# Three of four softmax-weight scalings moved from VectorE to GpSimd in a hybrid HGRN2/NSA decoder trunk

## The chip, the core and the metric

The kernel runs on one core of a Trainium2 chip, in float32 throughout. A core has a matmul engine (TensorE, PE in the profile, with its weight loads as PEld), VectorE (DVE), ScalarE (ACT), GpSimd (POOL), and SyncE (SP), which here only issues transfers. Each engine runs its own instructions in the order in which the program gives them, and waits on semaphores for what the others make. The metric is the device time of one execution in microseconds.

## The reference

Two layers, 512 tokens of width 1024. Each layer has a token mixer of two head groups (a gated linear recurrence, "HGRN2", and native sparse attention, "NSA"), an output product with a residual and a layer norm, and a SwiGLU feed-forward block with a second norm. The change lies in NSA. Cut to that:

```
for l in range(DEPTH):
    proj = x @ w_in[l]
    hq, hf, hi, hg, nq, kc, vc, ks, vs, kw, vw, gt = split(proj)
    o_a = hgrn2_mixer(hq, hf, hi, hg, ...)                 # 4 heads
    # NSA: 8 query heads, 2 key/value groups, gates g0, g1, g2 = sigmoid(gt) per head
    p_c = masked_softmax(q kc'^T * scale + bias)           # compressed blocks
    p_s = masked_softmax(q ks^T * scale + bias)            # selected blocks: all of them, as S = 512
    p_w = masked_softmax(q kw^T * scale + bias)            # sliding window
    o_b = g0 * (p_c @ vc') + g1 * (p_s @ vs) + g2 * (p_w @ vw)
    x = layer_norm(ALPHA * x + concat(o_a, o_b) @ w_out[l])
    x = layer_norm(ALPHA * x + (silu(x @ w_gate) * (x @ w_up)) @ w_down)
```

## The kernel before

Every large product is made of three fp32r products (a value is split into a rounded part and the rest: `whi`/`wlo`, `xh`/`xl`), at lines 82 to 84, with ScalarE making the rounded part and VectorE the rest (lines 76 and 77). These are most of TensorE's work.

NSA runs in 16 steps per layer (`nsa_all`): 8 heads times two branches, b = 0 for the selected blocks and b = 1 for the window. Of a step, `nsa_scores` makes the scores of four tiles of 128 tokens (qt = 0 to 3, 128, 256, 384 and 512 keys wide) on TensorE (lines 622 to 626, into `ps_s`), adds the bias from a strip and takes the minimum on VectorE (line 611), exponentiates and sums on ScalarE (line 613), and then makes the factor `sm`, one number per token and tile: the reciprocal of the sum (line 631) times the gate (line 632). The weights are scaled by it, three tiles on VectorE (line 635) and the widest on ScalarE (line 637). `nsa_pv` transposes the scaled weights on TensorE in groups of 4, 3 and 3 (line 652, into `ps_t`), ScalarE rounds each group (line 656), VectorE makes the rest (line 657), and TensorE multiplies both by the values (lines 662 and 663, into `ps_o`). `nsa_fin` ends a head.

The weights live in tiles named `e`: `e13` and `e2` of each step and `e0` of each head, two buffers each. So the scores of step i + 2 can be written by VectorE only when the transposes of step i are done.

Between the steps lie, called from `nsa_all` by step, other work: dense products with x (projections for the later heads and the linear recurrence, tiles `xh`, `xl`), the levels of the recurrence (`hg_levels`, with a GpSimd copy at line 392 on each level), its outputs (`hg_out`, lines 450 to 465, with a power on GpSimd at line 457), and at the end the first products of the output projection (`first_half`, `second_half`). GpSimd also issues transfers: the bias strips (line 328), residual rows (line 871), and sums of feed-forward weights (lines 104 and 105).

The order of the instructions on each engine is set when the program is built, by the tile framework's scheduler from priorities and its own estimates of durations; at run time nothing is reordered. A changed instruction can therefore move many others.

Of the kernel before, what the change touches and what calls it, by code (L numbers as in the profile page):

```python
# [13 lines left out]
OP = mybir.AluOpType  # L14
# [20 lines left out]
class Kern:  # L35
# [556 lines left out]
    def nsa_scores(self, h, b):  # L592
        nc = self.nc
        g = h // 4
        q = self.QS[h]
        KH, KL = self.KHL
        if b == 0:
            self.st = self.strip(h)
        st = self.st
        es = self.sb.tile([128, 1024], F32, name="e13", tag="e", bufs=2)  # L600
        e1, e3 = es[:, :512], es[:, 512:]
        e2 = self.sb.tile([128, 256], F32, name="e2", tag="e2", bufs=2)
        if b == 0:

            self.e0 = self.sb.tile([128, 128], F32, name="e0", tag="e0", bufs=2)
            self.mnsm = [(self.small(4, "mn"), self.small(4, "sm")) for _ in range(2)]
        E = [e1[:, 0:128] if b == 0 else self.e0, e2, e1[:, 128:512], e3]
        mn, sm = self.mnsm[b]

        def soft(e, pa, mn, sm):  # L610
            nc.vector.tensor_tensor_reduce(out=e, in0=pa, in1=st[:, 512 - pa.shape[-1]:], scale=1.0, scalar=3e38,  # L611
                                           op0=OP.add, op1=OP.min, accum_out=mn)
            nc.scalar.activation(e, e, AF.Exp, bias=mn, scale=-1.0, accum_out=sm)  # L613

        for qt in range(4):
            n = 128 * (qt + 1)
            qq = q[:, qt * 128:(qt + 1) * 128]
            if qt == 0:
                p0 = self.ps("s")
                if b == 0:  # L620
                    for i, k in enumerate((KH, KL)):
                        nc.tensor.matmul(p0[:, 256:], qq, k[:, g::2, :128], start=i == 0, stop=i == 1)
                continue
            p = p0[:, :n] if qt == 1 else self.ps("s")[:, :n]
            nc.tensor.matmul(p, qq, KH[:, 2 * b + g, :n], start=True, stop=False)
            nc.tensor.matmul(p, qq, KL[:, 2 * b + g, :n], start=False, stop=True)  # L626
            if qt == 1 and b == 0:
                soft(E[0], p0[:, 256:384], mn[:, :1], sm[:, :1])
                soft(self.e0, p0[:, 384:], self.mnsm[1][0][:, :1], self.mnsm[1][1][:, :1])
            soft(E[qt], p, mn[:, qt:qt + 1], sm[:, qt:qt + 1])  # L630
        nc.vector.reciprocal(sm, sm)
        nc.vector.tensor_tensor(sm, sm, self.gt[:, :, 8 * (b + 1) + h], op=OP.mult)
        for qt in range(4):
            if qt < 3:
                nc.vector.tensor_scalar(E[qt], E[qt], sm[:, qt:qt + 1], None, op0=OP.mult)
            else:
                nc.scalar.activation(E[qt], E[qt], AF.Copy, scale=sm[:, qt:qt + 1])
        self.E[h, b] = E
# [691 lines left out]
```

## Time and profile before

| | us |
|---|---|
| median of 3 runs | 1336.96 (1335.33 to 1340.11) |
| the profiled execution | 1336.99 |
| its span, first to last instruction | 1335.2 |
| TensorE busy in the span | 1303.4 (98%) |
| VectorE busy | 1015.6 (76%) |
| ScalarE busy | 748.0 (56%) |
| GpSimd busy | 186.5 (14%) |

The profiled execution's own time exceeds its span by 1.8 us. Its granted TensorE clock is 0.995 of full speed as a mean. In the profile a matmul's row is longer than the time until the next one may start, so a busy TensorE is not one at its peak. Engines run side by side, so the shares don't add up.

### The profile page before, as it was taken

The page shows a single profiled execution, that of the slowest core. Times are in us where ns is not written, and L with a number is a line of the kernel's source. Part 1 is how long each engine was busy: PE and PEld are TensorE (multiplying, and loading weights), DVE is VectorE, ACT ScalarE, POOL GpSimd, SP SyncE. Part 2 cuts the span into 40 slices and gives each one's busy share as a digit, 9 for nine tenths or more (in the row PEclk, how much of TensorE's full clock was granted, in tenths as well). Part 3 has the DMA queues.
Part 4 walks back from the last instruction along what each step waited for, and adds up shares of the span by engine and source line. Part 5 has one row for each costly group of instructions (what it writes and reads, how often), then busy time and mean ns, then how long its engine had stood idle before and what let it go on. Part 6 is the DMA issues. An engine that isn't in the chain of part 4 may idle for free.

```text
span 1335.2 us, 23431 instructions
## 1 busy us (share of the span) xinstructions
PE 1303.4 (98%) x8853; PEld 1197.8 (90%) x8853; DVE 1015.6 (76%) x2024; ACT 748.0 (56%) x1492; POOL 186.5 (14%) x267
## 2 busy tenths in 40 slices
PE   8999999999999999999999999998999999999997
PEld 6988999788999999888899989997899999998886
DVE  4755798867698777978758668988568887789777
ACT  5244787844655555645353558777356555556640
POOL 1140110110011212020011100101101112211102
PEclk9999999999999999999999999999999999999999
DMA  7253212162277888495433221123424778965952
GB/s 230 88 163 106 72 48 71 56 209 79 78 174 187 227 237 205 121 230 153 157 140 102 95 87 64 63 65 110 135 80 135 174 200 215 242 174 128 229 179 79
DMA packets 67554, 186.54 MB, mean 140 GB/s; under 512 B 8047, under 2 KB 8223, under 8 KB 66928
## 3 DMA queue, kind: packets, MB, share of 16 engines
q1 hardware_dynamic: 44640, 124.73, 28.1%
q0 software_dynamic: 21792, 58.47, 21.1%
q10 hardware_dynamic: 1008, 1.84, 0.4%
q8 instruction: 69, 1.13, 0.3%
q14 instruction: 45, 0.37, 0.1%
HBM read 180.76 MB, written 7.10 MB: 141 GB/s over the span
## 4 chain that ended last, share of the span: by engine, by line
PE 87%; DVE 5%; DMA 2%; ACT 2%; issue 2%; POOL 1%; POOLq 0%; DVEq 0%; ACTq 0%
PE ps_d L82 16%; PE ps_d L83 16%; PE ps_d L84 15%; PE ps_t L82 4%; PE ps_t L84 4%; PE ps_t L83 4%; PE ps_s L83 3%; PE ps_s L84 3%; PE ps_s L82 3%; PE ps_t L652 2%; PE ps_h L395 2%; PE ps_o L663 1%; PE ps_o L662 1%; PE ps_s L524 1%; PE ps_o L84 1%
## 5 line engine op out<-in xcount | busy, mean ns | idle before, releaser
L116 ACT CAST whi<-wraw 128x512 fp32r<-128x512 f32 x160 | 98.7, 621 | 127.5 <-PE ps_d L83 90.5
L117 DVE TENSOR_TENSOR wlo<-wraw,whi 128x512 fp32r<-128x512 f32 x160 | 109.2, 688 | 44.3 <-ACT whi L116 41.1
L84 PE MATMUL ps_d<-xh,wlo 128*128 128x256 f32 (+1 forms) x424 | 142.1, 336 | 0.0
L82 PE MATMUL ps_d<-xh,whi 128*128 128x256 f32 (+1 forms) x424 | 140.6, 336 | 1.5 <-ACT gates L502 1.1
L83 PE MATMUL ps_d<-xl,whi 128*128 128x256 f32 (+1 forms) x424 | 140.8, 333 | 0.0
L83 PE MATMUL ps_d<-tl,whi 128*128 128x256 f32 x480 | 135.0, 283 | 0.0
L84 PE MATMUL ps_d<-th,wlo 128*128 128x256 f32 x480 | 133.8, 283 | 0.0
L82 PE MATMUL ps_d<-th,whi 128*128 128x256 f32 x480 | 133.7, 283 | 0.0
L76 ACT CAST whi<-wraw 128x1024 fp32r<-128x1024 f32 (+1 forms) x68 | 70.8, 1041 | 104.2 <-PE ps_d L84 39.7
L77 DVE TENSOR_TENSOR wlo<-wraw,whi 128x1024 fp32r<-128x1024 f32 (+1 forms) x68 | 82.3, 1211 | 43.9 <-ACT whi L76 43.5
L83 PEld LDWEIGHTS ps_d<-tl,whi 128*128 128x128 f32 x480 | 92.1, 192 | 0.2
L82 PEld LDWEIGHTS ps_d<-th,whi 128*128 128x128 f32 x480 | 91.4, 192 | 0.2
L84 PEld LDWEIGHTS ps_d<-th,wlo 128*128 128x128 f32 x480 | 91.4, 192 | 0.0
L82 PEld LDWEIGHTS ps_d<-xh,whi 128*128 128x128 f32 x424 | 80.5, 192 | 8.9 <-ACT gates L502 1.3
L83 PE MATMUL ps_d<-wlo,xh 128*128 128x256 f32 (+1 forms) x304 | 88.3, 291 | 0.0
L82 PE MATMUL ps_d<-whi,xh 128*128 128x256 f32 (+1 forms) x304 | 88.0, 291 | 0.0
L84 PE MATMUL ps_d<-whi,xl 128*128 128x256 f32 (+1 forms) x304 | 87.8, 290 | 0.0
L84 PEld LDWEIGHTS ps_d<-xh,wlo 128*128 128x128 f32 x424 | 81.2, 192 | 7.0
L83 PEld LDWEIGHTS ps_d<-xl,whi 128*128 128x128 f32 x424 | 81.3, 192 | 6.5
L613 ACT ACTIVATE e<-e,mn 128x128 f32<-128x128 f32 (+3 forms) x128 | 71.7, 562 | 22.1 <-DVE mn L611 21.7
L611 DVE CUSTOM_DVE_ANT_0 e<-ps_s,strip 128x128 f32<-128x128 f32 (+3 forms) x128 | 59.1, 485 | 16.0 <-PE ps_s L626 12.9
L116 ACT CAST whi<-ws 128x512 fp32r<-128x512 f32 x80 | 49.5, 618 | 24.5 <-ACT sy L136 11.4
(460 smaller groups left out, 4179.0 us busy)
## 6 DMA issues: line engine op xcount, KB each, us to landing
wraw<-in_wd SPq DMA_DIRECT2D x36, 512.0 KB, 3.6
wraw<-in_wf SPq DMA_DIRECT2D x31, 512.0 KB, 3.2
wraw<-in_wg SPq DMA_DIRECT2D x24, 512.0 KB, 5.2
wraw<-in_wu SPq DMA_DIRECT2D x24, 512.0 KB, 5.0
ws<-in_wg SPq DMA_DIRECT2D x40, 256.0 KB, 4.0
ws<-in_wg POOLq DMA_DIRECT2D x40, 256.0 KB, 5.0
ws<-in_wu SPq DMA_DIRECT2D x40, 256.0 KB, 4.3
ws<-in_wu POOLq DMA_DIRECT2D x40, 256.0 KB, 6.3
```

Source lines behind the costliest of these rows:

```text
L76: nc.scalar.copy(h, raw[:, i:i + n])
L77: nc.vector.tensor_tensor(o, raw[:, i:i + n], h.bitcast(F32), op=OP.subtract)
L82: first = t.matmul(out, ah, bh, start=start, stop=False, **kw)
L83: t.matmul(out, ah, bl, start=False, stop=False, **kw)
L84: t.matmul(out, al, bh, start=False, stop=stop, **kw)
L116: nc.scalar.copy(h, raw)
L117: nc.vector.tensor_tensor(o, raw, h.bitcast(F32), op=OP.subtract)
L395: nc.tensor.matmul(p2[:, i], S[:, blk(i)], kq(128 * (i + 2), [[2 * w, n], [256 + w, 2], [1, w]]), start=True, stop=True)
L524: nc.tensor.matmul(ph[:, :62], w1[:, j * 128:(j + 1) * 128], U[half][:, j].rearrange("p g n -> p (g n)"), start=half == 0 and j == 0, stop ...
L611: nc.vector.tensor_tensor_reduce(out=e, in0=pa, in1=st[:, 512 - pa.shape[-1]:], scale=1.0, scalar=3e38, op0=OP.add, op1=OP.min, accum_out=mn)
L613: nc.scalar.activation(e, e, AF.Exp, bias=mn, scale=-1.0, accum_out=sm)
L652: nc.tensor.transpose(p[:, c:c + 128], E[qt][:, j * 128:(j + 1) * 128], self.ident)
```

## The change

The scaling of the tiles qt = 0, 1 and 2 of every step is given to GpSimd. ScalarE keeps qt = 3.

```
@@ nsa_scores
         for qt in range(4):
             if qt < 3:
-                nc.vector.tensor_scalar(E[qt], E[qt], sm[:, qt:qt + 1], None, op0=OP.mult)
+                nc.gpsimd.tensor_scalar(E[qt], E[qt], sm[:, qt:qt + 1], None, op0=OP.mult)
             else:
                 nc.scalar.activation(E[qt], E[qt], AF.Copy, scale=sm[:, qt:qt + 1])
```

The order moves on all engines within both mixer stages. Three places follow, all in the first layer; the second layer has the same order there.

TensorE in the kernel before, at the end of the dense products with x. `e_2164`, `e_2387` and `e_2388` are the weights of step 9 (counted from 0).

```order
L84 MATMUL ps_d<-whi,xl 128x256
L414 MATMUL ps_h<-hgKQ 128x128 x2
L662 MATMUL ps_o<-pth,vt 128x256
L663 MATMUL ps_o<-pth,vt 128x256
L662 MATMUL ps_o<-pth,vt 128x128
L663 MATMUL ps_o<-pth,vt 128x128
L584 MATMUL ps_s<-ident,cT 128x128 x4
L622 MATMUL ps_s<-kh,qs 128x256
L622 MATMUL ps_s<-kl,qs 128x256
L625 MATMUL ps_s<-kh,qs 128x256
L626 MATMUL ps_s<-kl,qs 128x256
L652 MATMUL ps_t<-ident,e_2164 128x128
```

TensorE in the changed kernel, at the end of the same dense products. `e_2162` and `e_2163` are the weights of step 8.

```order
L83 MATMUL ps_d<-wlo,xh 128x256
L84 MATMUL ps_d<-whi,xl 128x256
L560 MATMUL ps_s<-kc,qs 128x64 x8
L662 MATMUL ps_o<-pth,vt 128x384
L414 MATMUL ps_h<-hgKQ 128x128 x2
L663 MATMUL ps_o<-pth,vt 128x384
L652 MATMUL ps_t<-ident,e_2162 128x128
L662 MATMUL ps_o<-pth,vt 128x256
L652 MATMUL ps_t<-ident,e_2163 128x128
L663 MATMUL ps_o<-pth,vt 128x256
L662 MATMUL ps_o<-pth,vt 128x128
L663 MATMUL ps_o<-pth,vt 128x128
```

The last dense product with x stood before the transposes of step 9, and now stands before those of step 8. From it to the last transposes of step 15, TensorE's order holds 256 matmuls in the kernel before and 314 in the changed one; among the 58 more are 10 transposes, 10 products with the values, 6 score products, 12 products at line 560, and 18 products of the output projection.

TensorE at step 10 in the kernel before (`e_2466` and `e_2467` are its weights):

```order
L652 MATMUL ps_t<-ident,e_2466 128x128
L652 MATMUL ps_t<-ident,e_2467 128x128 x2
L652 MATMUL ps_t<-ident,e_2466 128x128 x4
L622 MATMUL ps_s<-kh,qs 128x256
L622 MATMUL ps_s<-kl,qs 128x256
L625 MATMUL ps_s<-kh,qs 128x256
L626 MATMUL ps_s<-kl,qs 128x256
L625 MATMUL ps_s<-kh,qs 128x384
L626 MATMUL ps_s<-kl,qs 128x384
L662 MATMUL ps_o<-pth,vt 128x512
```

and in the changed kernel:

```order
L652 MATMUL ps_t<-ident,e_2466 128x128
L652 MATMUL ps_t<-ident,e_2467 128x128 x2
L652 MATMUL ps_t<-ident,e_2466 128x128 x4
L662 MATMUL ps_o<-pth,vt 128x512
L663 MATMUL ps_o<-pth,vt 128x512
L662 MATMUL ps_o<-pth,vt 128x384
```

Six score products that stood between the transposes and the first product with the values have moved elsewhere. In the changed kernel's first layer the same neighbourhood, the seventh transpose and then at once the product with the values, is found at steps 9, 10, 12 and 14; before, at step 14 alone.

GpSimd in the kernel before, in the second half of the first layer's steps (`hgS` is the copy for a level of the recurrence, `rs` the power in `hg_out`):

```order
L392 COPY hgS<-hgKQ 128x256 x4
L333 DMA cstrip<-csd 128x448
L392 COPY hgS<-hgKQ 128x256 x2
L328 DMA strip<-Z 128x512 x3
L457 ISA
L457 TENSOR_TENSOR rs<-ss,mhalf 128x4 x2
L104 DMA ws_3773<-in_wg 128x512
```

and in the changed kernel, from step 8 on:

```order
L635 TENSOR_SCALAR e_2162<-e_2162,sm 128x128
L635 TENSOR_SCALAR e_2163<-e_2163,sm 128x256
L635 TENSOR_SCALAR e_2162<-e_2162,sm 128x384
L328 DMA strip<-Z 128x512 x2
L635 TENSOR_SCALAR e_2164<-e_2164,sm 128x128
L635 TENSOR_SCALAR e_2388<-e_2388,sm 128x256
L635 TENSOR_SCALAR e_2387<-e_2387,sm 128x384
L457 TENSOR_TENSOR rs<-ss,mhalf 128x4
L328 DMA strip<-Z 128x512
L635 TENSOR_SCALAR e_2466<-e_2466,sm 128x128
L635 TENSOR_SCALAR e_2467<-e_2467,sm 128x256
L635 TENSOR_SCALAR e_2466<-e_2466,sm 128x384
```

The scalings stand in GpSimd's queue among the strips' transfers and the powers. Further on, the three scalings of step 14 stand behind one weight sum (line 104), a power and four residual transfers (line 871).

## Rows read from the trace of the kernel before

**Rows 1.** The page: the span, and each engine's busy time with its share of the span and number of instructions.

```profile
span 1335.2 us, 23431 instructions
PE 1303.4 (98%) x8853; PEld 1197.8 (90%) x8853; DVE 1015.6 (76%) x2024; ACT 748.0 (56%) x1492; POOL 186.5 (14%) x267
```

**Rows 2.** Busy time of each engine in stretches of the span: from and to in us, length, then busy us and number of instructions of each engine, the granted clock, the share of the DMA engines, GB/s. 140 to 232 and 797 to 890 hold the NSA steps that have dense products with x beside them in layers 1 and 2; 232 to 282 and 890 to 942 hold those that have none.

```profile
core 0: us, PE busy (x) PEld busy (x) DVE busy (x) ACT busy (x) POOL busy (x), PEclk, DMA share, GB/s
140.00:232.00 92.00, 92.00 (x672) 86.88 (x670) 78.84 (x227) 71.27 (x160) 8.61 (x19) 1.00 0.21 67
232.00:282.00 50.00, 45.91 (x300) 38.49 (x299) 42.70 (x137) 41.44 (x126) 8.72 (x12) 1.00 0.35 106
797.00:890.00 93.00, 92.96 (x678) 87.67 (x677) 80.50 (x232) 71.84 (x161) 8.63 (x19) 1.00 0.21 67
890.00:942.00 52.00, 46.72 (x296) 39.47 (x295) 42.38 (x135) 41.87 (x125) 8.79 (x11) 0.97 0.35 102
```

**Rows 3.** TensorE's waits in 232 to 282 (first two) and in 890 to 942 (last two), by who ended them: total us, times, longest.

```profile
PE ps_o L662 <- ACT pth L656: 2.3, 2, 1.6
PE ps_h L462 <- DVE hy L459: 0.8, 3, 0.3
...
PE ps_o L662 <- ACT pth L656: 3.1, 3, 1.6
PE ps_o L663 <- DVE pth L657: 1.1, 3, 0.6
```

**Rows 4.** Groups by line, engine, operation and shape over the whole span: the three widths of line 635 on VectorE (busy us, mean ns of one, idle before).

```profile
L635 DVE TENSOR_SCALAR e<-e,sm 128x384 f32<-128x384 f32 x32 | 13.2, 413 | 0.0
L635 DVE TENSOR_SCALAR e<-e,sm 128x256 f32<-128x256 f32 x32 | 11.1, 347 | 0.0
L635 DVE TENSOR_SCALAR e<-e,sm 128x128 f32<-128x128 f32 x32 | 9.0, 283 | 0.6
```

**Rows 5.** GpSimd's compute: the copy of line 392 (least, median and greatest duration in ns), and the groups of a constant fill at line 303 and of the power at line 457 (busy us, mean ns).

```profile
L392 POOL COPY hgS<-hgKQ x56: 400/412/1520, 45.0 to 867.4; 128x256 f32<-128x256 f32 x56
L303 POOL MEMSET vz<- 128x512 f32 x1 | 0.6, 552 | 0.0
L457 POOL TENSOR_TENSOR rs<-ss,mhalf 128x4 f32<-128x4 f32 x8 | 8.9, 1114 | 31.8 <-DVE ss L455 19.8 <-DVE sm L632 12.0
```

**Rows 6.** Timeline of VectorE at the factors and scalings of step 13: start, duration, line and operation, number of instructions merged.

```profile
258.45 0.17 DVE L631 RECIPROCAL sm<-sm 128x4 f32<-128x4 f32 x1
258.65 0.17 DVE L632 TENSOR_TENSOR sm<-sm,gates 128x4 f32<-128x4 f32 x1
258.86 0.88 DVE L635 TENSOR_SCALAR e<-e,sm 128x128 f32<-128x128 f32 x3
```

**Rows 7.** The same of step 14, with what lies in between.

```profile
269.26 0.17 DVE L631 RECIPROCAL sm<-sm 128x4 f32<-128x4 f32 x1
269.35 0.99 DVE L657 TENSOR_TENSOR pth<-ps_t,pth 128x384 fp32r<-128x384 f32 x2
270.25 0.15 DVE L632 TENSOR_TENSOR sm<-sm,gates 128x4 f32<-128x4 f32 x1
270.33 0.68 DVE L611 CUSTOM_DVE_ANT_0 e<-ps_s,strip 128x512 f32<-128x512 f32 x1
270.94 0.08 DVE L611 DVE_READ_ACCUMULATOR2_ANT mn<- 128x1 f32 x1
270.94 0.28 DVE L635 TENSOR_SCALAR e<-e,sm 128x128 f32<-128x128 f32 x1
271.13 0.74 DVE L465 SCALAR_TENSOR_TENSOR y<-ps_h,sp,y 128x512 fp32r<-128x512 f32 x1
271.80 0.67 DVE L635 TENSOR_SCALAR e<-e,sm 128x256 f32<-128x256 f32 x2
```

**Rows 8.** Timeline of TensorE and VectorE: the last transposes of step 12, VectorE's first addition for step 14, the transposes of step 14 and the product that follows them, and its last transposes.

```profile
263.88 0.49 PE L652 MATMUL ps_t<-ident,e 128*128 128x128 f32 x3
264.41 0.29 DVE L611 CUSTOM_DVE_ANT_0 e<-ps_s,strip 128x128 f32<-128x128 f32 x1 [2.12 <-PE ps_t L652]
275.03 0.82 PE L652 MATMUL ps_t<-ident,e 128*128 128x128 f32 x6
276.50 0.50 PE L662 MATMUL ps_o<-pth,vt 128*128 128x512 f32 x1 [0.65 <-ACT pth L656]
277.74 0.49 PE L652 MATMUL ps_t<-ident,e 128*128 128x128 f32 x3
```

**Rows 9.** Timeline of VectorE and TensorE at step 5: its three scalings, and its first transpose.

```profile
191.66 0.87 DVE L635 TENSOR_SCALAR e<-e,sm 128x128 f32<-128x128 f32 x3
193.44 0.27 PE L652 MATMUL ps_t<-ident,e 128*128 128x128 f32 x1
```

**Rows 10.** Timeline of VectorE and GpSimd at the first `hg_out`: the line on VectorE that GpSimd's power waits for, and the power.

```profile
243.40 0.17 DVE L455 TENSOR_SCALAR ss<-ss 128x4 f32<-128x4 f32 x1 [0.77 <-ACT hy L454]
243.66 1.05 POOL L457 TENSOR_TENSOR rs<-ss,mhalf 128x4 f32<-128x4 f32 x1 [0.19 <-DVE ss L455]
```

**Rows 11.** Timeline of VectorE and GpSimd: a weight's remainder (two operands from SBUF) and a copy of line 392 that begins during it.

```profile
72.47 1.22 DVE L77 TENSOR_TENSOR wlo<-wraw,whi 128x1024 fp32r<-128x1024 f32 x1
72.69 1.26 POOL L392 COPY hgS<-hgKQ 128x256 f32<-128x256 f32 x1 [1.80 <-DVE hgKQ L427]
```

**Rows 12.** Groups of ScalarE in 232 to 282: the exponentials with their sums, and the rounding of the transposed weights.

```profile
L613 ACT ACTIVATE e<-e,mn 128x128 f32<-128x128 f32 (+3 forms) x24 | 13.5, 568 | 2.2 <-DVE mn L611 2.2
L656 ACT CAST pth<-ps_t 128x384 fp32r<-128x384 f32 (+1 forms) x20 | 9.8, 520 | 2.4 <-PE ps_t L652 2.2
L613 ACT ACTIVATION_READ_ACCUMULATOR e<-e,mn 128x1 f32 x24 | 4.8, 199 | 0.0
L676 ACT COPY ytmp<-ps_o 64x512 f32<-64x512 f32 x3 | 1.7, 583 | 0.1
```

More of the change, by code (lines that the diff above doesn't have):

```diff
@@ L634, in nsa_scores @@
             if qt < 3:
-                nc.vector.tensor_scalar(E[qt], E[qt], sm[:, qt:qt + 1], None, op0=OP.mult)
+                nc.gpsimd.tensor_scalar(E[qt], E[qt], sm[:, qt:qt + 1], None, op0=OP.mult)
             else:
```

## The prediction, made before the changed kernel ran

> **What bounds the kernel now.** I read the page first: TensorE is busy for 1303.4 of 1335.2 us [rows 1], so the matmuls are the bound nearly everywhere, and what VectorE or GpSimd do matters only where TensorE waits for them. So the next view is a table by stretch, to find where the steps that the change touches run and whether TensorE is full there [rows 2]. In 140 to 232 us and 797 to 890 us, where the dense products with x lie between the steps, TensorE has no idle time (0.04 us in 185). In 232 to 282 and 890 to 942, where those products are used up and the last seven steps run almost bare, it is idle for 4.1 and 5.3 us, and VectorE and ScalarE are busy 80 to 85% of the time. I call these the filled and the bare stretches.
>
> Busy TensorE is not TensorE at its peak, so the loss is better read from the weight loads: in the filled stretch they take 86.88 of 92 us (94.4%; 94.3% in layer 2), in the bare ones 38.49 of 50 and 39.47 of 52 [rows 2]. At the filled stretch's share the bare ones would last 38.49/0.944 = 40.8 and 39.47/0.943 = 41.9 us. So some **9.2 and 10.1 us** are lost there (in layer 2 the granted clock reads 0.97, in layer 1 1.00, so a part of the second loss may be the clock's), 19 us in all or 1.4%: the most that any change of these chains can win. TensorE's own waits there are named after ScalarE's rounding of the transposed weights (2.3 and 3.1 us) and VectorE's products (0.8, 1.1) [rows 3], never after the scaling itself: the scaling is upstream of them.
>
> **What the change removes.** 96 VectorE instructions, 32 of each width: 413 + 347 + 283 ns, 1.04 us a step, 33.3 us in all [rows 4]. In the filled stretches this is worth nothing, since TensorE is full there. In the bare ones it takes 7 x 1.04 = 7.3 us off each of VectorE's 42.7 and 42.4 us.
>
> **What it adds on GpSimd.** The trace has no such instruction there. Nearest is the copy of 128x256, one input and one output: 0.41 us in the median [rows 5]. Scaled by width, with the 552 ns fill of 512 as a hint of the slope [rows 5], the three are about 0.26 + 0.41 + 0.56 = **1.2 us** a step. Lower bound: the fill's rate for all, 0.55 x 768/512 = 0.8 us. Upper bound: a fixed price like the power's, 1.11 us for 4 columns [rows 5], three times, 3.3 us. I take 1.2, since reading a tile and writing it back is what the copy does. The hand-over costs 0.09 us (VectorE's line 455 ends at 243.57, GpSimd's power begins at 243.66) [rows 10]. GpSimd itself has room: 8.7 of 50 us are used [rows 2], and 8 steps would add 10.
>
> **What it does to one step's path.** With nothing in between, reciprocal to scaled weights takes 258.45 to 259.74 = 1.3 us [rows 6]; at step 14, where VectorE slips a rounding, an addition and another product in between, 269.26 to 272.47 = 3.2 us [rows 7]. On GpSimd it would be 0.4 to the end of the gate's product, 0.1 of hand-over and 1.2: 1.7 us, 0.4 longer than the free path and 1.5 shorter than the crowded one. So the path stays about as long as it is, and VectorE's queue is shorter for the others. In the filled stretches a later weight is covered: at step 5, the tightest, the scaling ends at 192.53 and the first transpose starts at 193.44 [rows 9], 0.9 us of slack, and meanwhile TensorE has dense products. Were that cover gone, 0.4 us at each of 9 steps would cost 3.6 us a layer.
>
> **What moves.** In the changed order the dense products end before the transposes of step 8, not of step 9 (first two excerpts), so a step more runs bare, with 314 matmuls from there to the last transpose, not 256. At the filled stretch's 92/672 = 0.137 us [rows 2], the 58 are 7.9 us of TensorE's work that leave the filled stretch or the stage behind. The total of the matmuls does not change, so the time changes by what the bare stretch loses: **its length less its work**. The work is then 40.8 + 7.9 = 48.7 and 41.9 + 7.9 = 49.8 us.
>
> Its length follows the busiest helper. ScalarE gets, by the order, 3 exponentials more (0.57 + 0.20 each), 3 roundings (0.52) and 3 single pieces like the copy of 0.58 [rows 12]: 5.6 us, less the 0.1 by which neighbouring rows overlap, some 5.0. It has then 46.4 and 46.9 us of work; VectorE has some 39 (42.7 less 7.3, and about 3.6 for the step). **ScalarE takes VectorE's place as the busiest.** If it is busy for the same share as now (41.44/50 = 0.829 and 41.87/52 = 0.805) [rows 2], the stretches last 46.4/0.829 = 56.0 and 46.9/0.805 = 58.3 us, and lose 7.3 and 8.5 where they lost 9.2 and 10.1: 1.9 + 1.6 = **3.5 us less**. That is my forecast, and it is small because the relief goes to an engine that hands the limit to another one. The profiled execution took 1336.99 us, span and what lies around it, practically the median of 1336.96; less 3.5 it is 1333.5, rounded 1334. If ScalarE reached the share that VectorE has now (0.854, 0.815), the loss would be 5.6 and 7.7: 6 us won.
>
> **A rule weighed.** A copy of 0.41 us took 1.26 us when it began 0.2 us into VectorE's remainder of a weight, an instruction with two operands in SBUF, and it ended 0.26 us after that one [rows 11]. The Trainium skill, SBUF — State Buffer, section Who interferes with whom, states it as a lock: a GpSimd instruction that reads SBUF and a VectorE one with two SBUF inputs exclude each other for their whole length. The trace agrees, and the rule speaks against the change. In a bare stretch such VectorE instructions are few (some 6 of 50 us, as line 77 is mostly in the filled ones); of 24 scalings about 3 would meet one and lose some 0.5 us, 1.5 us a layer if all were on the path. The forecast with it would be 1336 to 1337, without it 1334; I leave it in the range.
>
> **Rival: VectorE was the real limit (18%).** For it: 85% busy in layer 1, more than any other helper, with additions, remainders and products queued one behind another [rows 2, 7]. Freed of 7.3 us, it would hand ScalarE its work sooner; at a share of 0.88 the stretches last 52.7 and 53.3 us and lose 4.0 and 3.5: 11.8 us won, **1325**. Against it: TensorE's waits name ScalarE first [rows 3], and ScalarE at 0.88 would have to be fuller than any helper is now.
>
> **Rival: the loop over the weight buffers grows (27%), slower.** A weight tile has two buffers, so VectorE begins step 14 at 264.41, when step 12's last transpose has ended at 264.37, after 2.12 us idle [rows 8]; step 14's last transposes end at 278.23. A round is 13.9 us and holds two steps, whose scalings both lie in it. Four bare heads in two layers make 8 rounds. GpSimd's path, 0.5 us and the three scalings, is longer than the middle of the free and the crowded path, 2.25 us, when the three take more than 1.75 us; what they take beyond that counts twice a round. The 3.5 us won are gone at 0.44 us a round, with three scalings of 2.0 us. With 2.4 us, nearly halfway between my value and the power's price, a round grows by 1.3 us: 10.4 - 3.5 = 7 us lost, **1344**. It **decides from a mean of 0.66 us** for a scaling. For it speaks the new order: at steps 9, 10, 12 and 14 nothing stands between the seventh transpose and the product that needs its rounding, and at step 14 that place cost 0.65 us already [rows 8]. Against it the copy's 0.41 us [rows 5]. At the power's price, 3.3 us, some 21 us would be lost.
>
> The Trainium skill, GPSIMD Engine Reference, opening, calls GpSimd the wrong engine for plain elementwise work, VectorE being about twice as fast. No row here shows that for a scaling; by it the three would take 2.1 us, an estimate from that page, and the sum would be about 2 us lost.
>
> **Rival: nothing follows (7%).** The waits stay where they are, at ScalarE's rounding, and the longer bare stretch eats what the scaling gave: 1337.
>
> **How the numbers follow.** A difference under 0.3%, 4.0 us, is about what a measurement of this kernel can't tell from none. The forecast case has 48%: with shares of ScalarE between 0.78 (1.8 us lost) and the 0.854 of VectorE (6 us won) it spans 1331 to 1339; 20 of its 48 lie beyond 4 us won, 28 within. VectorE as the limit: 18, all faster. The loop: 24 slower, 3 within. Nothing: 7 within. Faster 0.38, same 0.38, slower 0.24. The range goes from the one rival's 1325 to the other's 1344; what is left out is a GpSimd at the power's price, and a ScalarE above 0.88.
>
> **What would show it.** Right: VectorE about 33 us less busy, GpSimd about 40 more; the three scalings near 0.26, 0.41 and 0.56 us; no new idle time of TensorE in the filled stretches; the dense products ending some 8 us earlier, and from there to the last transposes 56 to 58 us with ScalarE at 80 to 83%. Wrong: scalings above 0.66 us in the mean, or GpSimd's queue blocked by a transfer before a scaling; TensorE waiting for line 635; a bare stretch beyond 59 us; or ScalarE near 88%.

## The result: 9 us slower, and the profile after

The changed kernel takes 1345.94 us, the median of 7 runs (1343.84 to 1348.4), the kernel before 1336.96 (7 runs beside them): a ratio of 1.0075, 95% interval 1.0061 to 1.0089. That is 9.0 us by the medians and 10.0 by the ratio. The forecast was for less time than before; the result is more, and beyond the slow end of the forecast's range.

The page of the changed kernel, span and busy time as in [rows 1]:

```profile
span 1342.1 us, 23483 instructions
PE 1304.7 (97%) x8853; PEld 1195.8 (89%) x8853; DVE 998.9 (74%) x1928; ACT 742.8 (55%) x1488; POOL 286.1 (21%) x363
```

GpSimd is busy for 99.6 us more, not 40, VectorE for 16.7 less. The groups by shape tell why: the three scalings on GpSimd (busy us, mean ns of one, idle time before), beside VectorE's 413, 347 and 283 ns in [rows 4]:

```profile
L635 POOL TENSOR_SCALAR e<-e,sm 128x384 f32<-128x384 f32 x32 | 42.9, 1340 | 0.0
L635 POOL TENSOR_SCALAR e<-e,sm 128x256 f32<-128x256 f32 x32 | 30.9, 965 | 0.0
L635 POOL TENSOR_SCALAR e<-e,sm 128x128 f32<-128x128 f32 x32 | 22.6, 706 | 68.6 <-DVE sm L632 43.0 <-PE ps_t L652 20.8 <-ACT pth L656 4.5
```

A step's three take 3.01 us, 2.9 times VectorE's 1.04. In each layer three pairs of steps (10 and 11, 12 and 13, 14 and 15), all in the bare stretch, have their scalings one behind the other. GpSimd's timeline at steps 10 and 11 (start, duration, number merged):

```profile
245.18 0.64 POOL L328 DMA_DIRECT2D strip<-Z  x1 [7.38 <-DVE sm L632]
245.87 6.21 POOL L635 TENSOR_SCALAR e<-e,sm 128x128 f32<-128x128 f32 x6
252.06 1.05 POOL L457 TENSOR_TENSOR rs<-ss,mhalf 128x4 f32<-128x4 f32 x1
```

The stretches, cut to whole us at the last dense product with x and the last transpose of each layer (length; busy us of PE, PEld, DVE, ACT, POOL; clock). First the changed kernel, filled and bare in layer 1, then in layer 2:

```profile
140.00:224.00 84.00, 84.00 (x622) 79.72 (x621) 63.61 (x164) 60.41 (x141) 33.82 (x43) 1.00 0.20 63
223.00:287.00 64.00, 56.92 (x364) 46.93 (x364) 49.45 (x148) 49.49 (x143) 32.53 (x36) 1.00 0.32 99
801.00:884.00 83.00, 83.00 (x610) 78.64 (x608) 63.47 (x167) 59.26 (x138) 33.28 (x41) 1.00 0.21 64
885.00:949.00 64.00, 56.76 (x364) 46.83 (x363) 49.40 (x148) 49.40 (x143) 32.37 (x36) 1.00 0.33 99
```

Then the bare stretches of the kernel before, cut in the same way:

```profile
231.00:282.00 51.00, 46.91 (x307) 39.40 (x306) 43.70 (x140) 42.22 (x126) 8.72 (x12) 1.00 0.35 106
889.00:942.00 53.00, 47.68 (x302) 40.26 (x301) 43.38 (x137) 42.87 (x126) 8.79 (x11) 0.97 0.34 100
```

In the filled stretches TensorE still has no idle time. By the prediction's own measure, a bare stretch's length less its weight loads at the filled share of 0.944, before loses 51 - 39.40/0.944 = 9.3 and 53 - 40.26/0.944 = 10.4 us, together 19.6. The changed kernel loses 14.3 and 14.4: 28.7. The 9.1 us more are as much as the whole result. The spans of these two profiled executions differ by only 6.9 us (1335.2 and 1342.1), so some 2 us must have been won outside the bare stretches; where isn't shown. Three of TensorE's waits over the span, by who ended them (total us, times, longest):

```profile
PE ps_t L652 <- POOL e L635: 3.1, 6, 1.0
PE ps_o L662 <- ACT pth L656: 2.8, 6, 0.5
PE ps_s L584 <- DVE cT L575: 1.3, 2, 0.7
```

The first and third are new; the second was longer before, 2.3 + 3.1 us in [rows 3]. So there were two suspects, and the change brings both at once: **A**, GpSimd's price, and **B**, the order that the scheduler made for it.

### The profile page after: what moved, and what is told of

Same layout as the page of the kernel before. It is cut to its first block, busy times and chain, and to the rows that moved or that the text cites. A ratio compares the mean times of both kernels' runs of the same rounds, so it can differ in the third digit from the quotient of the medians.

```text
span 1342.1 us, 23483 instructions
## 1 busy us (share of the span) xinstructions
PE 1304.7 (97%) x8853; PEld 1195.8 (89%) x8853; DVE 998.9 (74%) x1928; ACT 742.8 (55%) x1488; POOL 286.1 (21%) x363
## 4 chain that ended last, share of the span: by engine, by line
PE 90%; DVE 5%; ACT 2%; DMA 1%; issue 1%; POOLq 0%; SPq 0%; DVEq 0%; ACTq 0%
PE ps_d L83 16%; PE ps_d L82 16%; PE ps_d L84 16%; PE ps_t L82 4%; PE ps_t L83 4%; PE ps_t L84 4%; PE ps_s L83 4%; PE ps_s L84 3%; PE ps_s L82 3%; PE ps_t L652 2%; PE ps_o L663 2%; PE ps_h L395 2%; PE ps_s L625 1%; PE ps_o L662 1%; PE ps_o L83 1%; PE ps_o L84 1%
## 5 line engine op out<-in xcount | busy, mean ns | idle before, releaser
L77 DVE TENSOR_TENSOR wlo<-wraw,whi 128x1024 fp32r<-128x1024 f32 (+1 forms) x68 | 83.1, 1221 | 50.9 <-ACT whi L76 50.5
L635 POOL TENSOR_SCALAR e<-e,sm 128x128 f32<-128x128 f32 (+2 forms) x96 | 95.1, 1004 | 68.6 <-DVE sm L632 43.0
L613 ACT ACTIVATE e<-e,mn 128x256 f32<-128x256 f32 (+3 forms) x128 | 71.4, 560 | 15.5 <-DVE mn L611 14.5
L392 POOL COPY hgS<-hgKQ 128x256 f32<-128x256 f32 x56 | 33.6, 603 | 174.7 <-DVE hgKQ L387 76.9
```

Source lines behind the costliest of these rows:

```text
L77: nc.vector.tensor_tensor(o, raw[:, i:i + n], h.bitcast(F32), op=OP.subtract)
L392: nc.gpsimd.tensor_copy(S.rearrange("p (n two w) -> p n two w", two=2, w=w), kq(0, [[2 * w, 2 * n], [768 + w, 2], [1, w]]))
L635: nc.gpsimd.tensor_scalar(E[qt], E[qt], sm[:, qt:qt + 1], None, op0=OP.mult)
```

## The experiments

### Price and order apart

In the next kernels every engine's instructions are chained in a written-out order, so that only one of the two differs. In the traces the rows of every engine, those of line 635 aside, stand in the same sequence as in the kernel that the order was taken from. A scaling's place on an engine that didn't have it in that kernel is left to the scheduler.

price_only (changed scalings, order of before):

```
-                nc.vector.tensor_scalar(E[qt], E[qt], sm[:, qt:qt + 1], None, op0=OP.mult)
+                nc.gpsimd.tensor_scalar(E[qt], E[qt], sm[:, qt:qt + 1], None, op0=OP.mult)
...
+        keep_order(nc, tc)
```

> The changed kernel's three scalings on GpSimd, but every instruction of all engines kept in the order of the kernel before (only the 96 scalings leave VectorE's row). Theory A (GpSimd's price: 3.0 us a step where VectorE took 1.04, twice in a round of the weight buffers, lengthens the bare stretches): slower, 1343 to 1348, about all of the 9.0 us. Theory B (the changed order: dense products used up a step earlier, so that a step more runs bare): about 1337, within 0.3% of before. If both matter, in between, 1339 to 1343.

order_only (VectorE's scalings, order of the changed kernel):

```
+        keep_order(nc, tc)
```

> The scalings stay on VectorE, and every instruction of all engines stands in the order of the changed kernel. Theory A: no slower than before, 1333 to 1339. Theory B: about 1346, as slow as the changed kernel.

Measured: price_only 1348.28 us, ratio 1.0086 (1.0069 to 1.0103); order_only 1344.55, ratio 1.0065 (1.0046 to 1.0084). Each theory had forecast that one of the two would be about as before. **Either part alone costs about what both cost together**: 11.5 and 8.7 us by the ratios, where both together cost 10.0. They don't add up.

TensorE's wait for the scalings in price_only, then two bare stretches: layer 1 of price_only and of order_only:

```profile
PE ps_t L652 <- POOL e L635: 10.6, 15, 1.3
```

```profile
229.00:286.00 57.00, 48.81 (x309) 39.73 (x308) 39.19 (x119) 42.82 (x127) 31.15 (x33) 1.00 0.30 96
```

```profile
222.00:286.00 64.00, 56.81 (x367) 47.25 (x365) 54.47 (x171) 49.60 (x144) 10.03 (x13) 1.00 0.32 99
```

In the order of before the late weights are waited for 15 times, 10.6 us. In the changed order 3.1 us are left of that, but the order is slow before GpSimd does anything: with VectorE's scalings the stretch lasts the same 64 us. That the scheduler chose this order because it reckoned with GpSimd's time is argued, not shown.

### Where the price is paid

The edit of both, with the order of before kept:

```
-                nc.vector.tensor_scalar(
+                (nc.vector if 2 * h + b < 8 else nc.gpsimd).tensor_scalar(
```

> Order of before; GpSimd makes the scalings of steps 8 to 15 of each layer alone (the last four heads), VectorE those of steps 0 to 7. Theory A with the cover of the dense products: all of the loss of price_only is here, 1343 to 1348. Rival C (a late weight costs the same at every step, covered or not): half of it, about 1341.

> Order of before; GpSimd makes the scalings of steps 0 to 7 of each layer alone (the first four heads, among dense products), VectorE those of steps 8 to 15. Theory A: within 0.3% of before, 1335 to 1339, since TensorE is full there. Rival C: about 1341.

bare: 1347.94 us, 1.0085 (1.0066 to 1.0104), all of price_only's loss from half of its scalings. filled (the two engines exchanged): 1339.05, 1.0019 (1.0006 to 1.0033), 2.5 us, and TensorE waits for line 635 for 0.5 us. Theory A's place is right in the main: beside dense products the late weight costs 2.5 us, without them 11.4.

### Is there a threshold?

narrow and two, in the order of before:

```
-                nc.vector.tensor_scalar(
+                (nc.gpsimd if qt == 0 else nc.vector).tensor_scalar(
```

> Order of before; GpSimd scales only the 128-wide tile (0.6 us at the changed kernel's minimum), beside VectorE, which keeps the other two (0.35 and 0.41 us). GpSimd's part, hand-over included, then ends about when VectorE's ends, and VectorE is rid of 0.28 us a step. If the loss goes by the path to the last scaled tile: no slower than before, 1334 to 1338. If the loss comes from each scaling that is on GpSimd (a third of price_only's 11.5): 1339 to 1341.

```
-                nc.vector.tensor_scalar(
+                (nc.gpsimd if qt < 2 else nc.vector).tensor_scalar(
```

> Order of before; GpSimd scales qt = 0 and 1 (128 and 256 wide: 0.64 + 1.09 = 1.73 us in the mean of price_only), VectorE qt = 2. The prediction's rule for the loop over the weight buffers put the point from which it costs at 1.75 us of scaling on GpSimd. By that rule: 1336 to 1338. If the loss goes with the columns that are on GpSimd (384 of 768, half of price_only's 11.5): 1341 to 1342.

narrow: 1336.7 us, 1.0005 (0.9994 to 1.0015), no change. two: 1342.65, 1.0052 (1.0034 to 1.0069), 6.9 us, near its second case. In two GpSimd's scalings took longer than I had reckoned:

```profile
L635 POOL TENSOR_SCALAR e<-e,sm 128x256 f32<-128x256 f32 x32 | 37.7, 1178 | 0.0
L635 POOL TENSOR_SCALAR e<-e,sm 128x128 f32<-128x128 f32 x32 | 24.5, 767 | 57.6 <-DVE sm L632 36.6 <-ACT e L613 15.4 <-PE ps_d L84 3.0
```

That is 1.95 us a step, 0.20 above the prediction's 1.75. By its rule (twice a round, 8 rounds) the loss would be 0.20 x 16 = 3.2 us; it was 6.9. price_only's three took 3.14 us and cost 11.5, where the rule gives 22. So the loss doesn't begin at 1.75 us: 6.9/1.95 and 11.5/3.14 are 3.5 and 3.7 us lost for each us that GpSimd needs in a step. Only narrow, whose GpSimd part (0.79 us) runs beside VectorE's other two, is below that line. An edge somewhere between 0.79 and 1.95 us isn't excluded.

### What in the order costs

Theory B1 says that the early end of the dense products does it, B2 that the rows of the bare stretch do. Two orders were joined, one from each kernel, at the last dense product of each layer:

```
+        keep_order(nc, tc)
```

> Scalings on VectorE as before. In each layer the order of before up to its last dense product with x (ahead of step 9's transposes), and from there on what is left in the order of the changed kernel. Theory B1 (the changed order costs its time because the dense products are used up a step earlier, and more work is left for the bare stretch): 1335 to 1338, as before. Theory B2 (the changed order costs its time by how it sets VectorE's, ScalarE's and TensorE's rows in the bare stretch itself): 1342 to 1345.

> The counterpart: scalings on VectorE; the order of the changed kernel up to its last dense product with x (ahead of step 8's transposes), and from there on what is left in the order of before. Theory B1: 1342 to 1345, as slow as the whole changed order with VectorE. Theory B2: 1335 to 1338.

> The order of late_fill, with the scalings on GpSimd. If GpSimd's price is hidden in the bare stretch by the changed order of that stretch (as it seems to be in the changed kernel, which is only about 1 us slower than its order with VectorE's scalings), this is within 2 us of late_fill. If the early use of the dense products is what hides it, it is as slow as price_only, 1346 to 1349.

late_fill: 1350.01 us, 1.0096 (1.0072 to 1.012). early_fill: 1348.02, 1.0089 (1.007 to 1.0108). late_fill_gpsimd: 1352.01, 1.0118 (1.0099 to 1.0137). **Inconclusive for B1 and B2**: both joints are slower than either whole order. The seam has a price of its own: in layer 1 of early_fill TensorE waits 2.7 us once for line 415, at the joint. And early_fill's bare stretches had a granted clock below full:

```profile
224.00:288.00 64.00, 56.32 (x346) 47.28 (x345) 53.39 (x168) 48.43 (x142) 9.90 (x14) 0.95 0.31 91
```

late_fill_gpsimd is 2 to 3 us above late_fill, near its first case: in the changed order of the bare stretch GpSimd's price is small, also where the dense products end late, but on a joint that is itself slow.

So the order was moved without a seam, by the scheduler itself. The next four ask for the last two groups of dense products earlier:

```
-            6: [(80, nq(3)), (80, alloc("V")), (80, tok(0, 0))],
-            7: [(80, tok(0, 1))],
+            6: [(80, nq(3)), (80, alloc("V")), (40, tok(0, 0))],
+            7: [(40, tok(0, 1))],
```

> The kernel before, with the last two groups of dense products (tok of steps 6 and 7) asked for a little earlier (offset 40 in place of 80), so that the scheduler itself sets another order, with scalings on VectorE and no seam. 257 matmuls then lie between the last dense product and the last transpose (before: 256; the changed kernel: 314). Theory B1 (the time follows the matmuls left for the bare stretch; 58 more cost 8.7 us for two layers, 0.075 us each): 1336, as before. Theory B3 (the order of before is one that fits well throughout, and nearly any other order of these rows costs some us, wherever the dense products end): slower by 3 us or more, 1339 to 1348.

> The same with offset 60: 280 and 287 matmuls in the bare stretches of the two layers. Theory B1: (24 + 31) x 0.075 = 4 us slower, 1340. Theory B3: slower by 3 us or more, in no order with the count of matmuls.

> The same with offset 20: 303 and 296 matmuls in the bare stretches. Theory B1: (47 + 40) x 0.075 = 6.5 us slower, 1342.5. Theory B3: slower by 3 us or more, in no order with the count of matmuls.

> The changed kernel (scalings on GpSimd) with offset 60 in place of 80: 354 and 353 matmuls in the bare stretches (314 in the changed kernel). Theory B1: 79 x 0.075 = 6 us slower than the changed kernel, 1351 to 1352. Theory B3: anything from 1342 to 1352.

prio40: 1333.92 us, 0.9978 (0.9963 to 0.9994). prio60: 1337.96, 1.0008 (0.9993 to 1.0022). prio20: 1337.97, 1.0005 (0.9991 to 1.0019). prio60_gpsimd: 1351.41, 1.0092 (1.0055 to 1.0129). B3 falls: three other orders are within 2 us of before or faster, and prio40 is the only version here that beats both kernels. B1 as a count of matmuls falls too: prio20 has 303 and 296 in its bare stretches and costs 0.7 us, where B1 gave 6.5, and prio60 costs 1.0 where it gave 4. prio60_gpsimd came out where B1 put it, at 1351 us, but B3's 1342 to 1352 holds that too. Part of those matmuls don't come from the filled stretch but from behind it: by the built orders, products of the output projection in the bare stretch are 18 in before, 51 and 44 in prio20, 36 in the changed kernel. Out of the filled stretch, because the products with x end earlier there, come 40 matmuls in the changed kernel and 14 in prio20. The changed kernel's 58, which the prediction treated alike, were 40 of the one kind and 18 of the other.

One place in the changed order can be tried by itself. TensorE in order_only, layer 1 (idle before, and who ended it):

```profile
235.98 0.66 PE L584 MATMUL ps_s<-ident,cT 128*128 128x128 f32 x4 [1.53 <-DVE cT L575]
238.01 0.52 PE L662 MATMUL ps_o<-pth,vt 128*128 128x512 f32 x1 [0.46 <-ACT pth L656]
240.04 0.50 PE L663 MATMUL ps_o<-pth,vt 128*128 128x512 f32 x1 [0.58 <-DVE pth L657]
```

The softmax of the second group's compressed weights (VectorE, lines 565 to 575) now falls into the bare stretch, and some 1.5 us of it are uncovered in each layer; before had no such wait. no_ct_wait takes away what makes it wait:

```
             nc.tensor.transpose(pt[:, qt * 128:(qt + 1) * 128],
-                                T[:, (3 - qt) * 4:(4 - qt) * 4].rearrange("p h n -> p (h n)"), self.ident)
+                                self.ident if g else T[:, (3 - qt) * 4:(4 - qt) * 4].rearrange("p h n -> p (h n)"), self.ident)
```

> order_only (scalings on VectorE, the changed kernel's order) with the four transposes of the second group's compressed weights (line 584) reading the identity in place of cT, so that TensorE doesn't wait for VectorE's chain that makes cT; the chain itself stays. It leaves out the second group's compressed weights. In order_only TensorE is idle for 1.53 us at that place in layer 1, the longest of its waits in the bare stretch. If the place is one of those that make up the order's 8.7 us: 3 us less than order_only, 1341 to 1342. If the wait only moves to the next late weight: as order_only, 1344 to 1346.

1344.79 us, 1.0069 (1.0051 to 1.0087): no gain. The same place:

```profile
234.87 0.60 PE L584 MATMUL ps_s<-ident 128*128 128x128 f32 x4
237.63 0.50 PE L662 MATMUL ps_o<-pth,vt 128*128 128x512 f32 x1 [1.24 <-ACT pth L656]
239.79 0.80 PE L663 MATMUL ps_o<-pth,vt 128*128 128x512 f32 x1 [0.58 <-DVE pth L657]
```

The wait moves to ScalarE's rounding a few rows on: 1.53 + 0.46 became 1.24. In this profile layer 1's stretch also had a clock of 0.92 (order_only 1.00), so what was won there may have been lost again. In layer 2, at a clock of 1.00 in both, the time from the last dense product to the last transposes is 62.4 us (885.82 to 948.23), order_only's 63.4 (883.75 to 947.15). So in this profile the place is worth 1.0 us in layer 2, and most of the order's loss lies elsewhere.

prio40_gpsimd puts the scalings of the changed kernel into the order of prio40:

```
-                nc.vector.tensor_scalar(E[qt], E[qt], sm[:, qt:qt + 1], None, op0=OP.mult)
+                nc.gpsimd.tensor_scalar(E[qt], E[qt], sm[:, qt:qt + 1], None, op0=OP.mult)
...
+        keep_order(nc, tc)
```

> All three scalings on GpSimd in the order of prio40, the one that was 2.8 us faster than before with scalings on VectorE. If GpSimd's price costs the same 11.5 us in any order that was made for VectorE's: 1344 to 1347. If an order that has more slack in the bare stretch hides it: 1334 to 1338.

1340.61 us, 1.003 (1.0015 to 1.0045): 6.7 us more than prio40, between the two expectations. So GpSimd's price isn't a constant: in this order it is a little over half of the 11.5 us that it was in the order of before. Of the kernels with all three scalings on GpSimd it is the fastest, and still slower than before.

### All runs by one measure

The loss of both bare stretches (length less weight loads/0.944), from one profile each, beside the ratio:

| kernel | lost in the bare stretches, us | ratio |
|---|---|---|
| prio40 | 14.8 | 0.9978 |
| prio40_gpsimd | 18.1 | 1.003 |
| before | 19.6 | 1 |
| filled | 20.8 | 1.0019 |
| narrow | 21.8 | 1.0005 |
| prio60 | 22.2 | 1.0008 |
| prio20 | 22.9 | 1.0005 |
| no_ct_wait | 25.7 | 1.0069 |
| two | 26.4 | 1.0052 |
| order_only | 27.9 | 1.0065 |
| changed | 28.7 | 1.0075 |
| early_fill | 29.0 | 1.0089 |
| prio60_gpsimd | 31.3 | 1.0092 |
| late_fill | 31.4 | 1.0096 |
| late_fill_gpsimd | 32.1 | 1.0118 |
| bare | 32.4 | 1.0085 |
| price_only | 32.7 | 1.0086 |

The time goes with this loss in the main (correlation 0.93 over the 17 rows), but not row by row: narrow, prio60 and prio20 lose 2 to 3 us more here than before and take about its time, and late_fill_gpsimd is the slowest without losing the most. As one profile each can show it, the bare stretches are the place. What stays open is how order_only's 8.7 us divide between the early end of the dense products and the rows of the bare stretch: the joints that should have told had prices of their own. Open, too, is why the two parts don't add up.

## Why the prediction was wrong

**What bounds the kernel** held. The changed kernel's filled stretches lost nothing, and the loss in the bare ones is as large as the result.

**GpSimd's price** is the first step that failed: what the prediction had as 0.26 + 0.41 + 0.56 = 1.2 us was 0.71 + 0.97 + 1.34 = 3.01 us. The bounds, 0.8 to 3.3, held it, but I took the value near the lower one, because a copy looked most like a scaling. The copy of 128x256 takes 0.41 us in [rows 5]; a scaling of the same shape took 0.97. The power's price, which I left out of the range, was the nearer row. The Trainium skill, GPSIMD Engine Reference, opening, has VectorE about twice as fast at elementwise arithmetic; the estimate of 2.1 us by it was nearer than mine, and the runs show 2.9 times.

**The path of a step** failed with it: 0.4 + 0.1 + 3.0 is 3.5 us, longer than the crowded path on VectorE (3.2), and with two steps in GpSimd's queue longer again. Step 11's reciprocal is this row, and its last scaling ends at 252.08 in the timeline above, 5.9 us later:

```profile
246.20 0.18 DVE L631 RECIPROCAL sm<-sm 128x4 f32<-128x4 f32 x1
```

**What moves** is the second step that failed, and it fails without GpSimd: order_only has the forecast's order with VectorE's scalings. The dense products ended 8.0 us earlier in layer 1 (231.2 to 223.2), as read from the order. The work that moved was sized about right: by the weight loads (46.93 - 39.40)/0.944 = 8.0 us and 7.0 in layer 2, where the prediction had 7.9. But "its length follows the busiest helper", at that helper's old share, gave 56.0 and 58.3 us; the changed kernel's stretches took 63.4 and 63.5 us from the last dense product to the last transposes. Two terms failed. The first is the helpers' work: ScalarE was busy for 49.49 us, not 46.4, and VectorE for 49.45, not "some 39". ScalarE rounds 26 groups where it had 20 [rows 12] and the prediction added 3. On VectorE the softmax of the compressed weights was left out, which comes along with the 12 products of line 560. Rows of the changed kernel in 223 to 287 (busy us, mean ns of one, idle before):

```profile
L656 ACT CAST pth<-ps_t 128x384 fp32r<-128x384 f32 (+1 forms) x26 | 12.8, 511 | 9.7 <-PE ps_t L652 9.4
L566 DVE TENSOR_TENSOR cT<-cT,cmn 128x512 f32<-128x512 f32 x1 | 0.7, 690 | 0.0
L569 DVE TENSOR_REDUCE cr<-cT 128x16 f32<-128x512 f32 x1 | 0.7, 686 | 0.1
L565 DVE TENSOR_REDUCE cmn<-cT 128x16 f32<-128x512 f32 x1 | 0.7, 678 | 0.0
```

With VectorE's scalings, in order_only, the stretch has 54.47 us of VectorE's work, 10.8 more than before's 43.70; the prediction added 3.6 for the step. So ScalarE didn't take VectorE's place; the two are equally busy. The second term is the share: 49.49 of 64 us is 0.77, not 0.83. With ScalarE's measured work the old shares give 59.7 and 61.4 us, so the work explains about half of the miss and the share the other half.

What a moved matmul costs can be estimated from the records of the trace, of which a product of lines 414, 418 or 450 makes two (the order's 256 matmuls of before are 302 records). A record takes 0.137 us in the filled stretch and, in before's bare ones, 50.5/302 = 0.167 and 52.9/302 = 0.175 (the second at a clock of 0.97). At that pace the 58 would cost 58 x (0.030 + 0.038) = 3.9 us, and the 40 that came out of the filled stretch 2.7; I booked the 58 as a gain of 3.5. That leaves more than half of order_only's 8.7 us to a bare stretch that runs slower than before's. For prio20's 14 the estimate is 1.0 us, and prio20 costs 0.7.

**The relief of VectorE** was smaller than 33 us: 1018.8 us in order_only, 998.9 in the changed kernel, and 22.2 less than before in price_only (993.4), whose order is that of before. The 33.3 us are the sum of rows that overlap their neighbours: in [rows 6] three take 0.88 us, not 1.04. What the relief bought isn't visible: VectorE's 54.47 busy us in the 64 of order_only fell to 49.45, with the same 64 us, but GpSimd's price came in the same step, and no run has the one without the other. The rival of VectorE as the real limit finds no support; that it was the limit in part isn't excluded.

**The rivals.** The loop over the weight buffers had the right direction and nearly the right time (1344 at 2.4 us), and its sign to look for, a mean above 0.66 us and TensorE waiting for line 635, appeared: 1.00 us and 3.1 us. Its formula is not confirmed, and that its time came near was luck: at 3.01 us it gives 1.26 x 16 - 3.5 = 16.7 us lost, two and price_only don't follow it, and in the changed kernel TensorE waits for the scalings for 3.1 us, where price_only has 10.6. The 21 us that it gave for the power's price were too many for the same reason.

**The rule weighed** shows again and is a small part. GpSimd's and then VectorE's rows at 191.25 us of the changed kernel, where line 681 reads two operands in SBUF:

```profile
191.25 1.14 POOL L635 TENSOR_SCALAR e<-e,sm 128x128 f32<-128x128 f32 x1
```

```profile
191.25 0.75 DVE L681 TENSOR_TENSOR y<-yv,y 128x512 fp32r<-128x512 f32 x1
```

The scaling took 1.14 us where the least is 0.60, and ended 0.39 us after VectorE's row. That agrees with the lock of the Trainium skill, SBUF — State Buffer, Who interferes with whom. A step's three take 2.73 us where none is longer than its least (162.10 to 164.83), so the lock's share in the mean of 3.01 is at most about 0.3 us a step. Nearly all of the price is there without it.

## What to carry to other kernels

Price an operation on another engine from a row of the same kind there, and where the trace has none, let the range reach to the dearest row of that engine, not to the most similar name. Where a scheduler answers a change with another order, time that order by itself, with the old operation in it: here it cost as much as the operation. Work that leaves a stretch where the matmul engine is full for one where it isn't runs at the second one's pace, and that is a loss to be booked (here 3 to 4 us, an estimate); and count for every helper all the work that comes with it, not the steps alone.

## What was not expected of the hardware

GpSimd's multiplication by one number per partition takes 0.60 us at the least for 128 columns and 1.24 for 384 (a row of three: 2.73 us), 2.5 ns a column; VectorE's mean goes from 283 to 413 ns, 0.5 ns a column. The gap grows with the width, from 2.1 times to 3.0.

The clock goes with most of what one kernel's times differ among themselves: over 75 runs of before, the time falls by 1.07 us for each 0.001 of mean granted clock (correlation -0.88), from a mean of 1339.8 us at 0.992 to 1333.6 at 0.997. In 12 of the 17 profiles the clock falls from its upper level (2.4 GHz) to its lower (1.2 GHz) in a bare stretch for a few us, besides falls elsewhere. In no_ct_wait the mean of a stretch of 8 us is 0.79 from 238 to 246 us, behind the waits shown above, and 0.66 from 278 to 286, each with a part at the lower level. The changed kernel's profile reads 1.00 in both bare stretches. Its median run had a mean clock of 0.993, before's profiled execution 0.995; by before's line that would be some 2 us of the difference, an estimate that no run tests.

```profile
238.00:246.00 8.00, 7.42 (x35) 6.18 (x35) 6.87 (x26) 5.60 (x17) 0.11 (x1) 0.79 0.01 2
278.00:286.00 8.00, 6.60 (x28) 5.47 (x29) 4.97 (x10) 3.14 (x6) 1.36 (x2) 0.66 0.71 189
```
